# Selection columns moved into the unused columns of another constant tile, and every page of SBUF 32 bytes lower

## The chip, the cores and the metric

The kernel runs on one core of a Trainium2 chip. A core has a matrix engine (TensorE, PE in the profile), a vector engine (VectorE, DVE), a scalar engine (ScalarE, ACT), a general engine (GpSimd, POOL) and a queue engine (SyncE, SP), which run side by side and wait for one another by semaphores, and 16 DMA engines that move data between HBM and SBUF. SBUF is the working memory: 128 partitions, each a row of bytes; a tile takes the same byte addresses in all its partitions. The metric is the device time of one execution in microseconds (us), as the median of several; ns are nanoseconds. A clock of 1.00 in a row of the profile is the full clock of the matrix engine, 0.50 half of it.

## What is computed

Two layers over 1024 latent tokens of width 1024 and 256 context tokens, in float32. Layer 0 is windowed attention (16 query heads, 4 key/value heads of 128, a window of 128 tokens to each side, all context keys and one sink logit in the same softmax), layer 1 a convolution module (three projections, a gate, a depthwise convolution of 31 taps, a layer norm, a projection back). Each layer has a modulation that comes from small vectors `c` and `c_ctx` through `ada_w`.

```python
shift, scale, gate = split(silu_c @ ada_w[i] + ada_b[i], 3)
h_lat = rmsnorm(x, norm_g[i]) * (1 + scale) + shift
# layer 0
proj = h_lat @ w_in                 # q, k, v and a gate path z
p = softmax([sink, q @ kc, q @ k_window])
y = ((p_ctx @ vc + p_win @ v) * silu(z)) @ w_out
# layer 1
a, gl, z = split(h_lat @ w_in + b_in, 3)
u = depthwise_conv31(a * sigmoid(gl)) + dw_b
y = (silu(layernorm(u)) * silu(z)) @ w_out
x = x + gate * y                    # after each layer; at the end rmsnorm(x)
```

## The kernel before

The large products are made with float32r operands. Each factor is split into a high part (a copy in float32r, by ScalarE) and a low part (the rest, by VectorE or GpSimd), and `mm3` (L196) adds three matmuls: high by high, high by low, low by high. Nearly all of them have 128 x 128 weights and a moving operand of 512 columns. In the profile's names the moving operand stands first: `psg<-hh_page,whi_page` streams 512 columns of `hh_page` past the weights `whi_page` into the PSUM tile `psg`.

The stages, in order of time: up to about 41 us the modulation weights, tokens and first weights are loaded and the first vectors made (the matrix engine partly fills with matmuls of zeros, `spin`, L306); to 100 us the first projections; to 830 us attention head by head, with the projections of the next head filled in between; to 1010 us the projection back of layer 0; to 1500 us the convolution layer (VectorE and GpSimd do the taps, while the matrix engine does its projections); then the projection back and the output.

Memory. `cpool` holds constants and small tiles, `pgpool` the working pages: 45 pages of 1024 floats and 6 half pages of 528 floats (`Pages`, L54; L114 and L115), which are given out and taken back as the program goes on. In the built program tiles are laid one behind the other in the order of their first use, each rounded up to 32 bytes. The constants begin like this:

```python
    ident = ctile([P, P], F32, "ident")      # L161, 512 bytes in each partition, at 1152
    vt = ctile([P, P], F32, "vt")            # L162, 512 bytes, at 1664
    sel = ctile([P, 2], F32, "sel")          # L163, 8 bytes, takes 32, at 2176
    sink = ctile([P, NH], F32, "sink")       # L164, 64 bytes, at 2208
```

`ident` and `vt` lie at multiples of 64 bytes. `sel` takes 32 bytes, and the tiles behind it are odd multiples of 32: `ones` at 2336, `dww` at 2848, `pthi` and `ptlo` (the transposed probabilities, and later the buffers of the convolution) at 4832 and 16096, and all 45 pages and 6 half pages. A page is 4096 bytes and a half page 2112 bytes (33 x 64), so all of them lie 32 bytes past a multiple of 64. Of the pages 26 lie 32 bytes past a multiple of 256, 9 at 96, 6 at 160 and 4 at 224. Slices of them that the matrix engine reads begin at multiples of 512 bytes from a page's start.

`sel` holds two columns of ones and zeros. It is loaded once (L298) and read by the matrix engine as a moving operand of 5 rows and 2 columns, 32 times in all, when the modulation is turned into columns (`ada_cols`, L413). `vt` holds the columns of several vectors: columns 96 to 111 are written from the norm weights (L325), columns 0 to 95 later (`turn_vecs`); columns 112 to 127 are not used.

What sets the order: the instructions are written out in a fixed order, with a scheduler that orders some of the engines' work from an estimate of times; each engine then runs its list in order, and waits for semaphores.

Of the kernel before, what the change touches and what calls it, by code (L numbers as in the profile page):

```python
# [9 lines left out]
F32 = mybir.dt.float32  # L10
# [4 lines left out]
P = 128  # L15
# [79 lines left out]
def backbone_kernel(  # L95
# [47 lines left out]
    def ctile(shape, dt, name):  # L143
        return cpool.tile(shape, dt, tag=name, name=name, bufs=1)
# [15 lines left out]

    ident = ctile([P, P], F32, "ident")  # L161
    vt = ctile([P, P], F32, "vt")  # L162
    sel = ctile([P, 2], F32, "sel")  # L163
    sink = ctile([P, NH], F32, "sink")  # L164
    nsink = ctile([P, NH], F32, "nsink")
    ones = ctile([P, P], F32, "ones")
# [1560 lines left out]
```

## Time and profile before

| what | before |
|---|---|
| median of 3 runs | 1757.55 us (1756.67 to 1760.27) |
| span of the profiled execution | 1752.9 us |
| median less span | 4.6 us |
| TensorE busy | 1720.7 us, 98% of the span |
| VectorE, ScalarE, GpSimd busy | 66%, 51%, 51% |
| DMA | 242.45 MB, mean 138 GB/s |

The span runs from the first to the last instruction of the profiled execution; the device time of a run has a few microseconds around it. Busy time of the matrix engine is the time in which at least one matmul is under way. Matmuls overlap one another, so what one of them costs is the step from its start to the start of the next, not its own length: a chain row such as `5.54 PE psg L89 x24` says that 24 matmuls follow one another in 5.54 us. All instructions have the line of a helper (L89), so the groups are told apart by their tiles.

### The profile page before, as it was taken

How to read it: one execution, taken by the hardware profiler on the slowest of the kernel's cores; microseconds unless marked ns; L12 is line 12 of the kernel's file. 1: busy time of each engine (PE TensorE's matmuls, PEld its weight loads, DVE VectorE, ACT ScalarE, POOL GpSimd, SP SyncE). 2: the span in 40 equal slices, each digit the busy share in tenths (PEclk: the TensorE clock that was granted, in tenths of full speed). 3: DMA queues.
4: the chain of work that ended last, by engine and by line, in shares of the span. 5: the costliest groups of instructions: out<-in, count | busy, mean ns of one | idle time of the engine just before them, and what ended most of it. 6: DMA issues, size and time to landing. Idle time of an engine off the chain costs nothing.

```text
span 1752.9 us, 23877 instructions
## 1 busy us (share of the span) xinstructions
PE 1720.7 (98%) x8420; PEld 1424.8 (81%) x8420; DVE 1148.3 (66%) x2079; ACT 889.4 (51%) x1548; POOL 895.4 (51%) x705
## 2 busy tenths in 40 slices
PE   7999999999999999999999999999999999999997
PEld 4788888888888888888888888888888888788886
DVE  6755564556546563656315189999999999867823
ACT  7555553445345444545334355554665564466731
POOL 0245654566636565653101267998898888130300
PEclk9999999999999999999999999999999999999999
DMA  9334443444334542436777733011121202377971
GB/s 313 107 82 139 136 133 85 145 147 145 100 105 143 152 142 87 136 119 203 279 250 239 241 90 105 13 54 31 43 79 36 91 30 79 120 254 243 325 264 48
DMA packets 195324, 242.45 MB, mean 138 GB/s; under 512 B 11798, under 2 KB 126790, under 8 KB 195204
## 3 DMA queue, kind: packets, MB, share of 16 engines
q1 hardware_dynamic: 188516, 230.10, 40.3%
q10 hardware_dynamic: 6688, 10.83, 2.6%
q8 instruction: 66, 1.08, 0.3%
q14 instruction: 54, 0.44, 0.1%
HBM read 188.70 MB, written 41.69 MB: 131 GB/s over the span
## 4 chain that ended last, share of the span: by engine, by line
PE 86%; DMA 5%; DVE 3%; POOL 2%; ACT 2%; issue 2%; SPq 1%; ACTq 0%; POOLq 0%; DVEq 0%
PE psg L89 44%; PE pss L89 22%; PE pso L89 19%; DMA araw_page<-in_ada_w_dram 1%; POOL rope_half L89 1%; DMA low_page<-in_conv_w_out_dram 1%; DMA rope_half<-rope_half 1%; SPq L89 1%; DMA low_page<-in_attn_w_out_dram 1%; DMA wolC<-low_page 1%; DVE mask_page L89 1%; ACT p_page L89 0%; POOL wlo_page L89 0%; POOL low_page L89 0%; DMA wraw_page<-in_attn_w_in_dram 0%
## 5 line engine op out<-in xcount | busy, mean ns | idle before, releaser
L89 POOL TENSOR_TENSOR odd_half<-odd_half,prod_half 128x513 f32<-128x513 f32 (+2 forms) x252 | 312.8, 1250 | 24.2 <-ACT prod_half L89 11.0
L89 PE MATMUL psg<-hh_page,whi_page 128*128 128x512 f32 x600 | 237.6, 396 | 0.0
L89 PE MATMUL psg<-hh_page,wlo_page 128*128 128x512 f32 x600 | 236.9, 395 | 0.0
L89 PE MATMUL psg<-hl_page,whi_page 128*128 128x512 f32 x600 | 236.8, 395 | 0.0
L89 POOL TENSOR_TENSOR wlo_page<-wraw_page,whi_page 128x1024 fp32r<-128x1024 f32 x70 | 173.1, 2475 | 104.1 <-ACT whi_page L89 83.2
L89 ACT ACTIVATE prod_half<-ubuf,dww 128x513 f32<-128x513 f32 (+2 forms) x252 | 165.1, 674 | 107.3 <-POOL odd_half L89 105.1
L89 POOL TENSOR_SCALAR p_page<-p_page,sc 128x640 f32<-128x640 f32 (+1 forms) x128 | 100.8, 787 | 224.4 <-DVE sc L89 208.7
L89 PE MATMUL psg<-h2h_page,whi_page 128*128 128x512 f32 x464 | 183.9, 396 | 0.0
L89 PE MATMUL psg<-h2h_page,wlo_page 128*128 128x512 f32 x464 | 183.0, 394 | 0.0
L89 PE MATMUL psg<-h2l_page,whi_page 128*128 128x512 f32 x464 | 182.4, 393 | 0.0
L89 DVE SCALAR_TENSOR_TENSOR pss<-ubuf,dww,pss 128x512 f32<-128x512 f32 (+3 forms) x270 | 172.3, 670 | 0.1
L89 DVE SCALAR_TENSOR_TENSOR pss<-ubuf,wsum,pss 128x512 f32<-128x512 f32 (+3 forms) x270 | 171.7, 670 | 0.2
L89 DVE TENSOR_TENSOR ptlo<-pss,pthi 128x640 fp32r<-128x640 f32 (+1 forms) x144 | 103.3, 717 | 64.0 <-ACT pthi L89 62.8
L89 ACT ACTIVATE p_page<-p_page,sc 128x641 f32<-128x641 f32 (+1 forms) x128 | 102.7, 802 | 74.1 <-DVE sc L89 69.7
L89 ACT ACTIVATE pthi<-pss 128x640 fp32r<-128x640 f32 (+1 forms) x144 | 88.6, 615 | 91.7 <-PE pss L89 86.3
L89 PEld LDWEIGHTS psg<-hh_page,wlo_page 128*128 128x128 f32 x600 | 112.9, 188 | 26.3
L89 PEld LDWEIGHTS psg<-hh_page,whi_page 128*128 128x128 f32 x600 | 113.0, 188 | 20.8 <-DVE kvc_page L89 0.2
L89 PEld LDWEIGHTS psg<-hl_page,whi_page 128*128 128x128 f32 x600 | 112.9, 188 | 20.7
L89 ACT ACTIVATE whi_page<-wraw_page 128x1024 fp32r<-128x1024 f32 x88 | 92.6, 1053 | 69.0 <-PE psg L89 25.5
L89 PE MATMUL pso<-h2l_page,whi_page 128*128 128x512 f32 x304 | 119.9, 394 | 0.0
L89 PE MATMUL pso<-h2h_page,whi_page 128*128 128x512 f32 x304 | 119.8, 394 | 0.0
L89 PE MATMUL pso<-h2h_page,wlo_page 128*128 128x512 f32 x304 | 119.6, 394 | 0.0
(244 smaller groups left out, 4105.2 us busy)
## 6 DMA issues: line engine op xcount, KB each, us to landing
wraw_page<-in_conv_w_in_dram SPq DMA_DIRECT2D x48, 512.0 KB
wraw_page<-in_attn_w_in_dram SPq DMA_DIRECT2D x40, 512.0 KB
wol_page<-wolA SPq DMA_DIRECT2D x32, 512.0 KB
wo_page<-in_attn_w_out_dram SPq DMA_DIRECT2D x32, 512.0 KB
wo_page<-in_conv_w_out_dram SPq DMA_DIRECT2D x32, 512.0 KB
wol_page<-wolC SPq DMA_DIRECT2D x32, 512.0 KB
rope_half<-rope_half ACTq DMA_DIRECT2D x80, 128.0 KB
araw_page<-in_ada_w_dram SPq DMA_DIRECT2D x32, 256.0 KB
```

Of the source, the lines that this page charges most:

```text
L89: r = f(*a, **k)
```

## The change

The tile `sel` is no longer made; the name now stands for two of the unused columns of `vt`. The load at L298 and the reads in `ada_cols` are written as before.

```diff
     ident = ctile([P, P], F32, "ident")
     vt = ctile([P, P], F32, "vt")
-    sel = ctile([P, 2], F32, "sel")
+    sel = vt[:, 112:114]
     sink = ctile([P, NH], F32, "sink")
     nsink = ctile([P, NH], F32, "nsink")
     ones = ctile([P, P], F32, "ones")
```

In the built program the instructions of every engine and of both DMA queues stand in the same order as before, with the same operands and the same semaphores waited for, but that `sel` reads `vt`. What differs is the addresses. `sel` is at 2112 in place of 2176, both multiples of 64. All tiles behind it lie 32 bytes lower: `sink` at 2176, `ones` at 2304, `dww` at 2816, `pthi` and `ptlo` at 4800 and 16064, and all 45 pages and 6 half pages at multiples of 64 bytes. Of the pages 26 are now at multiples of 256, 9 at 64 past one, 6 at 128 and 4 at 192. The distances between any two tiles behind `sel` are as before. Of the small tiles that follow `ptlo`, those that were at multiples of 64 are now 32 past one.

## The prediction

> **What bounds the kernel now.** I read the head of the page first, then the busy time by stage, the waits of the matrix engine and the chain of work that ended last.
>
> ```profile
> span 1752.9 us, 23877 instructions
> PE 1720.7 (98%) x8420; PEld 1424.8 (81%) x8420; DVE 1148.3 (66%) x2079; ACT 889.4 (51%) x1548; POOL 895.4 (51%) x705
> ```
>
> The matrix engine works for 98% of the span. By stage, with the columns window, its length, busy time and instructions of PE, PEld, DVE, ACT, POOL, the granted clock, the DMA share and GB/s:
>
> ```profile
> 0.00:41.00 41.00, 32.73 (x129) 18.48 (x129) 24.54 (x43) 29.83 (x36) 0.92 (x7) 0.96 0.98 310
> 100.00:830.00 730.00, 723.28 (x3992) 623.83 (x3991) 410.77 (x811) 353.60 (x754) 405.40 (x333) 1.00 0.43 129
> 830.00:1010.00 180.00, 180.00 (x834) 147.83 (x833) 52.70 (x102) 65.70 (x93) 24.27 (x26) 1.00 0.75 255
> 1010.00:1500.00 490.00, 488.51 (x2127) 396.69 (x2126) 463.35 (x752) 278.62 (x403) 407.88 (x300) 1.00 0.19 58
> 1500.00:1739.46 239.46, 239.41 (x1050) 194.68 (x1049) 148.29 (x275) 125.63 (x197) 42.58 (x28) 1.00 0.64 220
> ```
>
> From 100 us on it leaves out 8.3 us in 1639. Only the first 41 us are set by DMA (share 0.98); there the matrix engine spins on zeros. Its longest waits, and the chain in the convolution stage (start, length, what):
>
> ```profile
> PE pso L89 <- DVE alo_page L89: 4.7, 5, 2.2
> PE pss L89 <- DVE ptlo L89: 3.6, 2, 3.2
> ```
>
> ```profile
> 1169.76 5.57 PE pso L89 x24
> 1175.32 5.57 PE psg L89 x24
> 1180.89 5.54 PE pso L89 x24
> 1186.43 5.54 PE psg L89 x24
> ```
>
> Nothing waits here but for the matmul before. So the time of this kernel is the step from one matmul to the next, some 231 to 232 ns for 512 columns, times their number; and a change of addresses counts if it changes that step, or the first 41 us.
>
> **The change part by part.** *The tile that goes.* The instructions, their order and their waits are the same on every engine, so no instruction and no wait is added or taken away. The load and the readers of the selection columns:
>
> ```profile
> L89 PE MATMUL pso<-sel,arow_half x32: 245/247/268, 16.4 to 59.6; 5*128 5x2 f32 x32
> L89 SPq DMA_DIRECT2D sel<-in_k_sel_dram x1: 417/417/417, 2.4 to 2.4; - x1
> ```
>
> The DMA writes the same 8 bytes per partition, into another tile; the 32 small matmuls read from a multiple of 64 bytes before and after. Other columns of `vt` are written by VectorE, but no wait was added for that. I take 0, and the whole DMA issue, 0.4 us, is the most that it could give or cost.
>
> *VectorE and ScalarE at other addresses.* The taps of the convolution read the same buffer at starting points that move on by 4 bytes from one instruction to the next, so they cover nearly all places within 64 bytes. Durations as least/median/most, from 1160 to 1480 us:
>
> ```profile
> L89 ACT ACTIVATE prod_half<-ubuf,dww x163: 707/727/732, 1159.5 to 1477.9; 128x513 f32<-128x513 f32 x163
> L89 DVE SCALAR_TENSOR_TENSOR pss<-ubuf,wsum,pss x174: 476/744/750, 1162.8 to 1479.8; 128x512 f32<-128x512 f32 x168, 128x256 f32<-128x256 f32 x6
> ```
>
> The 163 ScalarE instructions lie within 3.4%, and the median stands near the top (the 476 of VectorE are its 256 columns). An address that is not a multiple of 64 costs these engines nothing that can be seen, and the matrix engine covers them: 0. GpSimd's reads are nearly all at one alignment, so it is not shown there; a gain or a loss of a few per cent is covered as well (it is busy for 408 of 490 us in its fullest stage).
>
> *DMA.* Where DMA sets the end, the chain has these pieces:
>
> ```profile
> 6.40 5.91 DMA araw_page<-in_ada_w_dram
> 15.91 7.07 DMA araw_page<-in_ada_w_dram
> 27.19 6.19 DMA araw_page<-in_ada_w_dram
> 33.40 5.10 DMA araw_page<-in_ada_w_dram
> ```
>
> Together 24.27 us. All pages lie 32 past a multiple of 64, so no row shows a large aligned transfer. For a bound I take the rate at a full share: 310 / 0.98 = 316 GB/s in the first stage against 255 / 0.75 = 340 between 830 and 1010 us, where rows are longer. If alignment were worth that whole 7%, 1.7 us would go; if it costs as much, 1.7 us come. Between such ends I take 0, since no row ties the rate to an address.
>
> *The matrix engine's reads.* This is the term that matters, and no large matmul of this trace has its moving operand at a multiple of 64. What can be seen is that the full clock is not used to the full. Matmuls of 512 columns at half clock (start, length) and the windows of that time, of a run of zeros, of a second such run, and of the convolution:
>
> ```profile
> 28.60 0.63 PE L89 MATMUL pss<-hh_page,wlo_page 128*128 128x512 f32 x1
> 29.03 0.63 PE L89 MATMUL pso<-ahi_page,c 128*4 128x512 f32 x1
> 29.46 0.63 PE L89 MATMUL pso<-alo_page,c 128*4 128x512 f32 x1
> 29.88 0.55 PE L89 MATMUL pso<-ahi_page,c 128*4 128x512 f32 x1
> ```
>
> ```profile
> 28.60:29.88 1.28, 1.28 (x4) 0.33 (x3) 1.28 (x2) 0.99 (x1) 0.00 (x0) 0.50 1.10 348
> 17.72:21.35 3.63, 3.63 (x18) 3.00 (x16) 2.44 (x10) 3.22 (x6) 0.00 (x0) 1.00 1.11 343
> 23.27:23.97 0.70, 0.70 (x4) 0.56 (x3) 0.00 (x0) 0.70 (x2) 0.00 (x0) 1.00 1.11 334
> 1100.00:1480.00 380.00, 380.00 (x1644) 308.81 (x1643) 365.39 (x540) 224.71 (x304) 338.12 (x238) 1.00 0.16 50
> ```
>
> A window's count takes in neighbours that reach into it; the weight loads (PEld) count the steps: 3 in 1.28 us is 427 ns at clock 0.50. Twice the clock would give 213.3. The convolution has 380.00 / 1643 = 231.3 ns, that is 18.0 ns or 7.8% more; the zeros had 3.63 / 16 = 226.9 at one time and 0.70 / 3 = 233 at another. So at the full clock the stream is held up by something, and other engines' work does not seem to be it: the steps are as long in the convolution, with VectorE at 96%, as between 830 and 1010 us with VectorE at 29%. Whether it has to do with the 32 bytes, this trace bears on at one place. The transposed probabilities are streamed in pieces of 128 columns that lie apart, each of 512 bytes and each beginning and ending in the middle of 64 bytes, and the queries in one piece:
>
> ```profile
> L89 PE MATMUL pss<-kh_page,ql_page 128*128 128x384 f32 x96 | 32.5, 339 | 0.0
> L89 PE MATMUL pso<-ptlo,vh_page 128*128 128x384 f32 x64 | 21.4, 335 | 0.0
> ```
>
> Three pieces touch 27 stretches of 64 bytes, one piece of 384 columns 25, and the three pieces are not slower (335 against 339 ns, length of one). Torn ends thus cost nothing that can be seen. What stays possible is that each 64 bytes within the stream cost more for being read across a boundary; I take 0 for it, as the row nearest to the question speaks for 0, and keep both ends: 18.0 ns less for each 512 columns, and 2 ns more (231.3 to the 233 of the second run of zeros).
>
> [...]
>
> *The sum.* 1752.9 + 0 + 0 + 0 is the span; the median of the runs stands 4.6 us above it. Forecast: 1757.5 us, and within no change 1754 to 1761.
>
> **The rivals.** *First: the 32 bytes are what holds the stream up, and it goes wholly.* For: the excess is there at the full clock only, and every stream lies off a multiple of 64. Against: the pieces above. The price goes by stage. In the attention stage some of the time is transposes:
>
> ```profile
> L89 PE MATMUL pss<-ident,p_page 128*128 128x128 f32 x608 | 87.2, 273 | 0.5 <-POOL p_page L89 0.5
> 92.99 0.44 PE pso L89 x4
> ```
>
> These take 0.44 / 4 = 0.11 us a step, just over twice 213.3 / 4, so they hardly suffer; 608 of them are 67 us, and 656 remain. A step of a transpose is 3 ns over its 106.7, and I leave as much on each matmul: 15 of 231.3 ns, 6.5%, would go. That is 43 us in attention, 12 in 830 to 1010, and 16 behind 1500. In the convolution it would be 32, but VectorE is busy for 463 of 490 us and becomes the bound; I take 18. In all 89 us: 1668. Without the 3 ns it would be 7.8% and 27 us at most in the convolution: 51 + 14 + 19 + 27 = 111 us, 1646, the utmost.
>
> [...]
>
> *Second: part of it goes.* The run of zeros at 226.9 ns shows that the same addresses allow 1.9% less than 231.3. If every stream went that well, (656 + 180 + 489 + 239) x 1.9% = 30 us: 1728. For: it has been seen. Against: the second run of zeros, at the same addresses, had 233, so it is not the address alone.
>
> [...]
>
> **How the numbers follow.** No change has 0.38: nothing but addresses moves, and the two engines whose reads can be told apart by address show no regard for it. The first rival has 0.22 and the second 0.20, since the excess of 18 ns is real and has no cause in the trace. The third has 0.20, for the same reason. A measurement of this kernel can tell about 0.2% from no change. Faster is 0.42, same 0.38, slower 0.20. The range reaches from 1660, just below the first rival, to 1766; what lies out are the worse part of the third rival and the utmost of the first, 0.17 together.
>
> **What would show it.** Steps in the convolution (380.00 us in 1643 weight loads): 231.3 says no change, 227 the second rival, 216 the first, with VectorE near 100% and waits of the matrix engine on it; 233 the third. The four DMA pieces at 24.3 us within 1.7. ScalarE's 727 ns and VectorE's 744 stay. The forecast is wrong if the step moves by 0.5 ns or more, or if a wait of the matrix engine appears that is not in the list.

## The result and the profile after

| | before | after |
|---|---|---|
| median, 20 runs each | 1756.84 us (1753.52 to 1760.51) | 1754.92 us (1751.98 to 1757.54) |
| ratio | | 0.9992 (0.9985 to 0.9998) |
| span of the profiled execution | 1752.9 us | 1753.0 us |

The time is the same within the 0.2% that can be told from no change. Inside that bound there is a small gain of 1.9 us in the medians, whose interval ends just short of 1. A second comparison gave 0.9989 (0.998 to 0.9997).

The head of the page after, and its stages, with the columns as in the prediction (window, length, PE, PEld, DVE, ACT, POOL, clock, DMA share, GB/s):

```profile
span 1753.0 us, 23877 instructions
PE 1721.8 (98%) x8420; PEld 1423.6 (81%) x8420; DVE 1142.9 (65%) x2079; ACT 890.2 (51%) x1548; POOL 896.3 (51%) x705
```

```profile
0.00:41.00 41.00, 33.69 (x129) 18.74 (x129) 25.18 (x44) 29.61 (x36) 0.92 (x7) 0.92 0.97 313
830.00:1010.00 180.00, 180.00 (x834) 147.62 (x834) 52.89 (x103) 65.10 (x93) 24.25 (x26) 1.00 0.74 255
1010.00:1500.00 490.00, 488.51 (x2127) 396.11 (x2126) 463.13 (x752) 278.61 (x403) 408.41 (x300) 1.00 0.19 58
1100.00:1480.00 380.00, 380.00 (x1643) 308.35 (x1642) 365.27 (x539) 224.50 (x304) 338.04 (x238) 1.00 0.16 50
```

In these two stages as many matmuls go through as before: 834 of 834 in the projection back of layer 0, 2127 of 2127 in the convolution. (From 100 to 830 us there are 3985 against 3992; in other profiles of the two kernels that number goes from 3988 to 4003.) The step in the convolution is 380.00 / 1642 = 231.4 ns; it was 231.3. The chain in the convolution reads as it did:

```profile
1169.55 5.57 PE pso L89 x24
1175.12 5.57 PE psg L89 x24
1180.68 5.54 PE pso L89 x24
1186.22 5.54 PE psg L89 x24
```

The other engines' instructions there (least/median/most in ns), and the load and the readers of the selection columns:

```profile
L89 ACT ACTIVATE prod_half<-ubuf,dww x163: 707/726/734, 1159.3 to 1477.7; 128x513 f32<-128x513 f32 x163
L89 DVE SCALAR_TENSOR_TENSOR pss<-ubuf,wsum,pss x174: 471/745/755, 1162.6 to 1479.6; 128x512 f32<-128x512 f32 x168, 128x256 f32<-128x256 f32 x6
L89 PE MATMUL pso<-vt,arow_half x32: 246/246/267, 17.2 to 57.7; 5*128 5x2 f32 x32
L89 SPq DMA_DIRECT2D vt<-in_k_sel_dram x1: 417/417/417, 2.4 to 2.4; - x1
```

726 against 727 ns, 745 against 744, 246 against 247, 417 against 417. And the pieces of DMA in the chain of the first 41 us:

```profile
6.41 5.79 DMA araw_page<-in_ada_w_dram
15.46 6.84 DMA araw_page<-in_ada_w_dram
28.95 5.96 DMA araw_page<-in_ada_w_dram
35.84 5.29 DMA araw_page<-in_ada_w_dram
```

Together 23.88 us, 0.39 less than before.

### The profile page after: what moved, and what is told of

The parts are those of the page before. It is cut to its first block, busy times and chain, and to the rows that moved or that the text cites. A ratio compares the mean times of both kernels' runs of the same rounds, so it can differ in the third digit from the quotient of the medians.

```text
span 1753.0 us, 23877 instructions
## 1 busy us (share of the span) xinstructions
PE 1721.8 (98%) x8420; PEld 1423.6 (81%) x8420; DVE 1142.9 (65%) x2079; ACT 890.2 (51%) x1548; POOL 896.3 (51%) x705
## 4 chain that ended last, share of the span: by engine, by line
PE 84%; DMA 6%; DVE 3%; POOL 2%; issue 2%; ACT 2%; SPq 1%; ACTq 0%; POOLq 0%; DVEq 0%
PE psg L89 43%; PE pss L89 21%; PE pso L89 19%; DMA araw_page<-in_ada_w_dram 1%; DMA rope_half<-rope_half 1%; POOL rope_half L89 1%; DMA wraw_page<-in_attn_w_in_dram 1%; SPq L89 1%; DMA low_page<-in_conv_w_out_dram 1%; DMA low_page<-in_attn_w_out_dram 1%; POOL wlo_page L89 0%; DMA x_page<-in_x_dram 0%; DVE mask_page L89 0%; DMA wolC<-low_page 0%; DMA wo_page<-in_conv_w_out_dram 0%
```

## The experiments

Three questions were left. Is the matrix engine's step deaf to every address, or only to this shift? What does its excess over 213 ns (the 427 ns at clock 0.50, halved: an estimate) consist of? And where do the two microseconds come from?

**The changed kernel again, and the 32 bytes put back.** The first is the changed kernel, run again. The second adds an unused tile of 32 bytes, so that every page is where it was before, while the selection columns stay in `vt`.

> The changed kernel itself, beside the runs that follow. If the 0.08% between it and the kernel before is real: ratio 0.9985 to 0.9998 again. If it is the scatter of the runs: 1.000 within 0.0007. In both, the step of a 512-column matmul in the convolution stays at 231.3 ns (380 us in 1642 or 1643 weight loads between 1100 and 1480 us).

```diff
     sel = vt[:, 112:114]
+    pad = ctile([P, 8], F32, "pad")
```

> The selection columns stay in the other tile, and an unused tile of 32 bytes puts every later tile back to where it was (pages 32 bytes past a multiple of 64). If addresses give the small gain: ratio to the kernel before 1.000, and the DMA pieces of the first 41 us as before (24.3 us). If the merging of the tiles gives it: 0.999. If it was scatter: 1.000 here and in the changed kernel alike. Step 231.3 ns by every theory.

The changed kernel had 1754.17 us against 1755.98, ratio 0.9989 (0.998 to 0.9997); with the 32 bytes put back 1756.37, ratio 1.0 (0.9991 to 1.0009). The convolution with the bytes put back:

```profile
1100.00:1480.00 380.00, 380.00 (x1643) 308.86 (x1642) 365.22 (x541) 225.61 (x307) 337.93 (x239) 1.00 0.16 50
```

1642 loads, as with the changed kernel. So the two addresses give the same step, and moving `sel` by itself gives nothing within 0.09%. If the gain of 0.1% is real, it goes with the addresses, though not with the step.

**Half of the pages off, and all of them off by 4 bytes.** The pages are made 32 bytes longer and used from an offset on. With offset 0 they alternate between multiples of 64 (24 of 45) and 32 past one; with one float they lie 4 bytes past a multiple of 32.

```diff
-        t = self.pool.tile([P] + list(shape or [self.words]), dt, tag=f"{self.tag}{i}",
-                           name=f"{name}_{self.tag}_{self.count}", bufs=1)
+        t = self.pool.tile([P, self.words + SLACK], dt, tag=f"{self.tag}{i}",
+                           name=f"{name}_{self.tag}_{self.count}", bufs=1)[:, OFF:OFF + self.words]
+        if shape and len(shape) > 1:
+            names = "abc"[:len(shape)]
+            t = t.rearrange(f"p ({' '.join(names)}) -> p {' '.join(names)}", **dict(zip(names[1:], shape[1:])))
```

`SLACK` is 8; `OFF` is 0 in the first kernel and 1 in the second. The first is thus the control of the second: the pages lie as far apart, and only the 4 bytes differ.

> Pages of 4128 bytes in place of 4096 (the last 32 not used), so that 24 of 45 lie at a multiple of 64 and 21 at 32 past one: the control of the next run, and a mixture of both alignments in one trace. If addresses do not matter to the matrix engine: steps of 231 to 232 ns whether the stream is from one sort of page or the other, ratio 0.999 to 1.001. If 32 bytes mattered to it in any way: two groups of steps more than 1 ns apart.

> The same pages, used from their fifth byte on, so that every page lies 4 bytes past a multiple of 32 and no stream, load or packet begins at a multiple of 16. My theory (the matrix engine does not care where a stream begins): step 231.3 ns within 0.5, ratio to the kernel before 0.999 to 1.002. Rival (lines of 16 bytes, which 32 and 64 do not test): each stream crosses one line more in every 16 bytes or at its ends, step 232 to 240 ns, ratio 1.003 to 1.04. For DMA: if packets care for alignment, the first 41 us grow by 1 us or more and the packets' share of the first stage rises; if not, they stay.

The first had 1758.73 us, ratio 1.0009 (0.9998 to 1.002). The second had 1784.62, ratio 1.0155 (1.014 to 1.0171): 27 us slower by the ratio, 25.9 by the medians of the two. The convolution of the first, and then of the second:

```profile
1100.00:1480.00 380.00, 380.00 (x1640) 307.55 (x1639) 365.50 (x540) 224.86 (x305) 337.20 (x239) 1.00 0.16 49
```

```profile
1100.00:1480.00 380.00, 380.00 (x1609) 303.85 (x1608) 360.10 (x536) 219.12 (x301) 332.39 (x241) 1.00 0.16 47
```

With 4 bytes the step is 380.00 / 1608 = 236.3 ns, 4.9 longer than in the changed kernel and 4.5 longer than in the control (380.00 / 1639 = 231.9). The profile has 5993 matmuls of 512 columns with 128 x 128 weights; 5993 x 4.5 ns = 27 us, which is the loss. The control itself has 1639 loads, where all ten profiles with the pages of the kernel before or of the changed kernel have 1642 or 1643: with other distances between the pages the step is some 0.4 ns longer, and no run shows why. So the matrix engine does heed the address of its operands, only not in steps of 32 bytes.

**The stream by itself.** Groups of 24 equal matmuls behind the changed kernel's own work, in one execution of each kernel; nothing reads their results. Each operand has a page of its own, at a multiple of 64. The first kernel varies the kind of stream:

```diff
+        def group(mov, wt, rows=P):
+            for _ in range(24):
+                PE.matmul(o[0:rows], wt, mov, start=True, stop=True)
+        group(m["warm"][:, 0:512], w[:, 0:P])
+        group(m["base"][:, 0:512], w[:, 0:P])
+        group(m["four"][:, 1:513], w[:, 0:P])          # 4 bytes on
+        group(m["late"][:, 8:520], w[:, 0:P])          # 32 bytes on
+        group(m["narrow"][:, 0:512], w[:, 0:4], 4)     # 4 columns of weights
+        group(m["strided"][:, 0:1024:2], w[:, 0:P])    # every second float
+        group(m["same"][:, 0:1].to_broadcast([P, 512]), w[:, 0:P])
+        group(b[:, 0:512], wb[:, 0:P])                 # bfloat16
```

> The changed kernel with 192 matmuls more at its end, whose results are not used: eight groups of 24, each streaming 512 columns of a tile of its own past weights of 128 columns. After a group that warms up the clock: from a multiple of 64; 4 bytes past it; 32 bytes past it; past weights of 4 columns only; every second float; the same float 512 times; and in bfloat16. My theory (the stream at full clock is held up by how fast float32r operands can be read, whatever the address): 231 ns within 3 in the first three, 231 with narrow weights, 460 or so with every second float if lines are what is read, under 220 with the same float 512 times, 216 in bfloat16. Rival (weights loaded in between hold it up): 231 in the first three, 214 to 220 with narrow weights. Rival (alignment holds it up): 214 to 220 from a multiple of 64, 231 or more in the other two. Rival (something behind the array, the writing of 4-byte results): 231 in all but bfloat16, and there too.

The matrix engine's timeline there (start, length of the whole group; each name ends in the operand's):

```profile
1745.60 5.76 PE L90 MATMUL pss<-benwarm_page,benw_page 128*128 128x512 f32 x24
1751.20 5.76 PE L90 MATMUL pss<-benbase_page,benw_page 128*128 128x512 f32 x24
1756.80 5.92 PE L90 MATMUL pss<-benfour_page,benw_page 128*128 128x512 f32 x24
1762.56 5.76 PE L90 MATMUL pss<-benlate_page,benw_page 128*128 128x512 f32 x24
1768.15 5.72 PE L90 MATMUL pss<-bennarrow_page,benw_page 128*4 128x512 f32 x24
1773.70 11.04 PE L90 MATMUL pss<-benstrided_page,benw_page 128*128 128x512 f32 x24
1784.55 5.44 PE L90 MATMUL pss<-bensame_page,benw_page 128*128 128x512 f32 x24
1789.83 5.35 PE L90 MATMUL pss<-benhalf_page,benv_page 128*128 128x512 bf16 x24
```

From start to start, divided by 24: 233 ns in the first group as in the second, so no warming of the clock shows; 233 at a multiple of 64 and 233 at 32 bytes past it, 240 at 4 bytes; 231 with 4 columns of weights; 452 where every second float is read; 220 where one float is read over and over. For bfloat16 the next start is missing; if its last matmul reaches as far beyond the next start as in the first two groups (5.76 - 5.60 = 0.16 us), it has 5.19 / 24 = 216 ns, an estimate. So most of the excess over 213 goes with reading different floats: 13 of some 20 ns go when the address stands still (220 for 233), and all but about 3 with operands of half the size (216, the estimate). It is not the writing, since the groups at 220 and at 216 write the same tile of 4-byte results as those at 233. Loading fewer weight columns gives 2 ns at most (231 for 233).

The next two kernels vary the place. One has 8, 12 and 16 bytes, weights moved by 4 bytes, and 256 columns side by side and 16 bytes apart:

> Eight groups of 24 matmuls stand behind the changed kernel's own work; nothing reads their results, and the time of the whole is longer by them. From the start of one group to the start of the next, divided by 24: streams of 512 columns at 0, 8, 12 and 16 bytes past the start of a page, then the first of these again with its weights 4 bytes past the start of a page, then 256 columns one after the other, and 256 columns of which each lies 16 bytes behind the last. Theory (the stream is read in stretches of 16 bytes): 233 ns at 0 and at 16 bytes, 240 at 8 and 12; weights at 4 bytes leave 233; 256 columns take 117, and with 16 bytes between them four times as many stretches are read, 4 x 117 = 468 at the utmost. Rival (stretches of 32 bytes): 240 at 16 bytes as well, and the last group no more than twice the group before it. Rival (the weights carry the loss at 4 bytes): 240 in the group with the moved weights.

```profile
1747.78 5.76 PE L90 MATMUL pss<-benbase_page,benw_page 128*128 128x512 f32 x24
1753.38 5.76 PE L90 MATMUL pss<-beneight_page,benw_page 128*128 128x512 f32 x24
1758.98 5.71 PE L90 MATMUL pss<-bentwelve_page,benw_page 128*128 128x512 f32 x24
1764.53 5.78 PE L90 MATMUL pss<-bensixteen_page,benw_page 128*128 128x512 f32 x24
1770.15 5.74 PE L90 MATMUL pss<-benbase_page,benv_page 128*128 128x512 f32 x24
1775.72 2.99 PE L90 MATMUL pss<-benfour_page,benw_page 128*128 128x256 f32 x24
1778.55 5.75 PE L90 MATMUL pss<-benstrided_page,benw_page 128*128 128x256 f32 x24
```

In this order: 233, 233, 231, 234, 232 with moved weights, 118 for 256 columns, and about 233 for 256 columns that lie 16 bytes apart (again with 0.16 us taken off). Weights moved by 4 bytes cost nothing (232 for 233). My theory that the engine fetches stretches of 16 bytes and pays for each of them fails at two places: 8 and 12 bytes lose nothing, and columns 16 bytes apart cost 0.91 ns each, hardly more than the 0.88 of columns 8 bytes apart. The other kernel asks for the period:

> Eight groups of 24 matmuls behind the changed kernel's own work, their results read by nothing: streams of 512 columns that start 0, 4, 12, 20, 28 and 36 bytes past the start of a page (a multiple of 64), 4 bytes again in another page, and 128 columns that lie 32 bytes apart. Start to start, divided by 24. Theory (4 bytes past a multiple of 32 is the place that costs): 240 ns at 4, 36 and again at 4, and 231 to 234 at 0, 12, 20, 28. Rival (4 past a multiple of 16): 240 at 20 too. Second rival (an odd multiple of 4 past 8): 240 at 12, 20 and 28 too, so that the 231 seen at 12 was an accident. Third rival (the 240 belonged to one page, whatever the offset): 232 at the second group with 4. The last group, by columns that stand apart at 0.89 to 0.91 ns each: 116 ns; by stretches of 16 or 32 bytes that are longer to reach: more.

```profile
1742.47 5.76 PE L90 MATMUL pss<-benwarm_page,benw_page 128*128 128x512 f32 x24
1748.06 5.92 PE L90 MATMUL pss<-benfour_page,benw_page 128*128 128x512 f32 x24
1753.82 5.72 PE L90 MATMUL pss<-bentwelve_page,benw_page 128*128 128x512 f32 x24
1759.38 5.88 PE L90 MATMUL pss<-bentwenty_page,benw_page 128*128 128x512 f32 x24
1765.10 5.70 PE L90 MATMUL pss<-entwentyeight_page,benw_page 128*128 128x512 f32 x24
1770.64 5.84 PE L90 MATMUL pss<-benthirtysix_page,benw_page 128*128 128x512 f32 x24
1776.32 5.83 PE L90 MATMUL pss<-benagain_page,benw_page 128*128 128x512 f32 x24
1781.99 2.82 PE L90 MATMUL pss<-benstrided_page,benw_page 128*128 128x128 f32 x24
```

At 0: 233 ns; at 4, 20, 36 and again 4: 240, 238, 237 and 236; at 12 and 28: 232 and 231. The first rival holds: what counts is the place within 16 bytes. Four past a multiple of 16 costs 3 to 7 ns, twelve past it saves 1 to 2. The two groups at 4 bytes differ by 4 ns between themselves, so one or two ns in a single group prove little; what 12 bytes are worth is for the whole kernel to show. The last group, 128 columns that lie 32 bytes apart, has about 112 ns (0.12 us taken off), 0.88 ns a column: a wider distance is not dearer. The expectation for it was 116.

**The best place, in the kernel.** The same edit with `OFF` 3 and with `OFF` 7, so that all pages lie 12 and 28 bytes past a multiple of 32. The control is again the kernel with `OFF` 0.

> As the kernel with pages 4 bytes past a multiple of 32, but 12 bytes past it. Theory (only 4 bytes past costs): steps of 512 columns of 231.7 ns and the time of the kernel before, ratio 0.999 to 1.001. Rival (any start that is no multiple of 16 costs): steps of 236 and ratio 1.015 as at 4 bytes.

> As the kernel with pages 12 bytes past a multiple of 32, but 28 bytes past it, which is 12 past a multiple of 16 too. Theory (the matrix engine's streams repeat every 16 bytes, and 12 past a multiple of 16 is their best start): steps of 512 columns of 230.0 ns on the mean, 1654 weight loads in the 380 us of the convolution, ratio 0.994 as at 12 bytes. Rival (12 bytes past a multiple of 32 is a place of its own): 231.7 ns, 1643, ratio 1.000. Second rival (the gain at 12 bytes had another cause than the streams, such as the start-up or the transfers): ratio below 0.997 with steps of 231.7 ns, or 1.000 with steps of 230.0.

At 12 bytes 1746.7 us, ratio 0.9943 (0.993 to 0.9957); at 28 bytes 1748.17, ratio 0.9951 (0.994 to 0.9963). The first, which was expected to change nothing, and then the second:

```profile
PE 1712.4 (98%) x8420; PEld 1426.3 (82%) x8420; DVE 1142.9 (65%) x2079; ACT 888.3 (51%) x1548; POOL 895.4 (51%) x705
1100.00:1480.00 380.00, 380.00 (x1655) 311.34 (x1654) 366.65 (x544) 224.22 (x304) 341.07 (x239) 1.00 0.17 50
```

```profile
PE 1709.6 (98%) x8420; PEld 1422.7 (81%) x8420; DVE 1149.8 (66%) x2079; ACT 888.9 (51%) x1548; POOL 897.4 (51%) x705
1100.00:1480.00 380.00, 380.00 (x1657) 310.98 (x1656) 367.99 (x543) 223.61 (x303) 340.90 (x239) 1.00 0.17 52
```

Steps of 380.00 / 1654 = 229.7 and 380.00 / 1656 = 229.5 ns, 1.7 and 1.9 below 231.4. With 5993 of them that is 10 and 11 us. Against the control the steps are 2.1 and 2.3 ns shorter and the medians 12.0 and 10.6 us. The busy time of the matrix engine fell by 9.4 and 12.2 us against the changed kernel, and the medians by 9.3 and 8.7 against the kernel before. Some of it is given back: span less busy time is 1747.9 - 1712.4 = 35.5 and 1746.6 - 1709.6 = 37.0 us, against 31.2 in the changed kernel. These are the fastest kernels of this study.

**Where the two microseconds come from.** The first profiles of both addresses parted at one place. In the start-up the matrix engine waits for the low part of a modulation page (a matmul of the third set, `pso<-alo_page,c`). Before, this wait was 2.21 us and ended at 43.09; the clock then fell to 0.50 for 3 us. In the two first profiles of the changed kernel it was 1.4 to 1.5 us, ended at 42.4, and the clock stayed at 1.00. That is some 2 us by 50 us, the size of the gain. Two tests: eight further matmuls in the kernel before, meant for this gap, so that the engine isn't idle there (their result is read by nothing), and one more profile of each kernel.

```diff
                 for n, (c, r) in enumerate(parts):
+                    if (pr, i, k, n) == (1, 2, 0, 1):
+                        fill = ps_o(1)
+                        for _ in range(8):
+                            PE.matmul(fill[0:4], c[:, 2 * i + k, :], parts[0][1][:, k], start=True, stop=True)
```

> The kernel before, with eight further matmuls of the second set of modulation rows in the gap of 2.21 us that the matrix engine has at 40.9 to 43.1 us; their result is read by nothing, and every other instruction is as before. Theory (the gap brings the clock down): the clock stays at 1.00 between 41 and 52 us, no step of 427 ns is left between 43 and 48 us, the wait ends at 43.1 as before, and what follows is 1.3 us earlier: the median is 1.3 us below the kernel before if the lead is kept to the end (ratio 0.9993), and equal if waits further on take it. Rival (the clock falls for another reason, at its own time): 0.5 between 44 and 47 us as before, ratio 1.000. Second rival (the changed addresses alone make the lead): the clock stays up, but the time is not below that of before.

> The kernel before, a second time, to see whether its start-up is the same in another execution. Theory (pages at 32 past a multiple of 64 bring the third set of transfers in later): the wait of the matrix engine for the low part of the third page ends at 43.1 to 43.3 us, as in both kernels with such pages so far, and the clock falls to 0.5 behind it. Rival (chance, from one execution to the next): it ends anywhere from 42.0 to 43.3, and the clock falls only where it ends late.

> The changed kernel, a third time, as a partner of the kernel before in the same hour. Theory (addresses): the same wait ends at 42.4 us, as in its two profiles so far, and the clock stays at 1.00. Rival (chance): anywhere from 42.0 to 43.3.

The eight matmuls did not come into the gap. The condition names the second set, and the gap stands in the third. In the matrix engine's timeline of that kernel, the matmuls added to the second set, and the end of the wait:

```profile
32.66 2.24 PE L89 MATMUL pso<-ahi_page,c 128*4 128x512 f32 x9
44.51 0.39 PE L89 MATMUL pso<-alo_page,c 128*4 128x512 f32 x1 [1.05 <-DVE alo_page L89]
```

So this run is no test of a filled gap. The time was 1758.14 us, ratio 1.0013 (1.0002 to 1.0024): 2.1 us more, about what eight steps of 0.23 us come to. The clock stayed at 1.00 behind the wait, which was 1.05 us here, and yet no time was won.

The kernel before, in its second profile: the end of that wait in the matrix engine's timeline, and the window behind it.

```profile
42.36 0.39 PE L89 MATMUL pso<-alo_page,c 128*4 128x512 f32 x1 [1.60 <-DVE alo_page L89]
44.00:47.00 3.00, 3.00 (x17) 2.33 (x15) 2.76 (x4) 3.00 (x6) 1.30 (x1) 1.00 1.01 397
```

The changed kernel, in its third:

```profile
43.19 0.40 PE L89 MATMUL pso<-alo_page,c 128*4 128x512 f32 x1 [2.49 <-DVE alo_page L89]
44.00:47.00 3.00, 3.00 (x8) 1.65 (x7) 1.95 (x4) 2.38 (x4) 1.29 (x1) 0.50 1.02 403
```

The roles are exchanged: this time the kernel before was early and kept its clock, and the changed kernel was late and lost it. The theory falls; this wait differs from one execution to the next. It doesn't set the end either: the changed kernel's third profile, with the late start, has the shortest span of the three, 1750.9 us. And a start-up at the full clock is not yet a run at the full clock. In the first profile of the changed kernel, which kept it there, the clock fell for 3.4 us later on; the same window in the first profile of the kernel before stands below it:

```profile
590.00:593.40 3.40, 3.40 (x10) 2.73 (x10) 2.23 (x4) 2.60 (x6) 3.40 (x3) 0.50 0.27 77
590.00:593.40 3.40, 2.11 (x11) 1.93 (x12) 2.67 (x7) 3.30 (x7) 1.60 (x2) 1.00 0.16 45
```

The kernel before had the same fall in its second profile; the mean granted clock is 0.995 in both profiles. Over all runs the mean granted clock is alike: 0.9962 in 29 runs of the kernel before, 0.9964 and 0.9963 in 20 and 11 of the changed kernel.

So the cause of the 0.1% stays open. It isn't the step of the matrix engine, it isn't the start-up wait, and it is hardly the clock (0.0002 of 1753 us is 0.4 us). One thing does go with the addresses: the transfers from SBUF to SBUF (queue q10) took 2.6 to 2.7% of the span in four profiles with pages at 32 past a multiple of 64, and 2.5% in the three of the changed kernel; the mean time of their 5120 packets of 2048 bytes was 137 to 141 ns and 131 to 133 ns. Those for `rope_half` have some 1% of the chain that ended last, 18 us; 4% of that is under 1 us, an estimate, so they could give a part of it. Whether the matrix engine's waits in the attention stage follow from that, single profiles can't tell, since their spans scatter by 3 us (1750.9 to 1753.9 for the changed kernel).

## Why the prediction was right, and where its reasons were not

*The forecast.* 1757.5 us with no change; 1754.92 came, inside 1754 to 1761 and with a ratio within 0.2% of 1. No change was the forecast but had a chance of only 0.38, against 0.42 for faster. The 4.6 us added to the span were too many: in every run on record the time is 1.7 to 1.9 us above the span of the same execution. The rest came of setting the profiled execution, a fast one, against the median of others.

*The tile that goes: 0.* The load stayed at 417 ns and the readers at 246; with the 32 bytes put back the ratio was 1.0. Right.

*VectorE and ScalarE: 0.* 745 against 744 ns and 726 against 727. Right. Even pages 4 bytes off a multiple of 32 left VectorE's busy time in its scatter (1147.0 us against 1142.9 to 1149.8 elsewhere), as far as such a sum can say.

*DMA: 0, within 1.7 us.* The four pieces took 23.88 us for 24.27. Right in size for the loads, and with pages 4 bytes past a multiple of 32 the first 41 us still moved 308 GB/s, against 310 before and 313 after. That no row ties a transfer to an address was true of the one trace; the packets from SBUF to SBUF, which the sum left out, became some 4% shorter (137 to 141 ns before, 131 to 133 after).

*The matrix engine's reads: 0.* 231.4 against 231.3 ns. Right, and for the reason given from the torn pieces: beginning and ending inside 64 bytes cost nothing there (335 against 339 ns). The reason given with the chances was too wide: that VectorE and ScalarE "show no regard" for an address was taken to speak for the matrix engine, which does show regard, with 4.9 ns lost at 4 bytes past a multiple of 16 and 1.7 to 1.9 gained at 12. The change was neutral as both 0 and 32 are multiples of 16: the streams at 0, 16 and 32 bytes took 233, 234 and 233 ns.

*First and second rival (1668, 1728).* The first gave the whole excess of 18 ns to the 32 bytes, the second a part of it. The step moved by 0.1 ns. In the groups the excess goes with reading different floats, at every address: 220 ns with one float and about 216 with bfloat16. Together they had 0.42, more than the forecast itself; that was the misjudged part of the prediction. The best address found takes off less than 2 of the 18 ns.

*Third rival (1769).* Each step was to go from 231.3 to the 233 ns of the second run of zeros, 11 us in all, since the reads of a stream and of the next weights would meet more often. That was the author's supposition, which had 0.20 and bears on the upper end of the range, 1766; no run shows such meetings. The step stayed at 231.4 ns, and weights moved by 4 bytes left 232 ns. The distances between pages do not change here; in the kernel where they do (`OFF` 0) the step is 231.9 ns, though whether weights and stream meet there is not shown.

*What would show it.* The list of signs named steps of 231.3, the DMA pieces and the two durations; all stood as listed for no change. A step of 229.5, which two of these kernels have, lay between the signs for no change and for the second rival, and the prediction had no case for it.

## What to carry to other kernels

Where the chain is one matmul behind the other, price a change of addresses by the step, counted as weight loads in a fixed window; 24 equal matmuls behind the kernel's own work show a difference of several ns in one profile (240 against 233 here), before anything is moved. In this kernel the start of the float32r streams within 16 bytes was what counted (steps of 231.4 ns at 0, 236.3 at 4, 229.7 at 12), and a shift by 32 bytes gave 0.1 ns; try 12. And before a difference between two profiles is made a cause, take each kernel's profile again: here a wait that explained the gain to the microsecond had changed sides. And look in the trace where an added instruction ran, before its result is read: here eight of them stood in another gap than the one they were meant for.

## What the runs showed of the hardware

- At the full clock, a float32r stream of 512 columns took 231 to 234 ns at 0, 8, 12, 16 and 32 bytes past a multiple of 64, 236 to 240 ns at 4 past a multiple of 16, and 220 ns with one float repeated. In the whole kernel, pages at 12 past a multiple of 16 gave 229.5 to 229.7 ns. Why 12 is best, no run shows.
- Columns 8, 16 and 32 bytes apart took 0.88, 0.91 and 0.88 ns each (452 ns for 512, 233 for 256, 112 for 128), against 0.45 for neighbours (233 for 512).
- In the start-up the matrix engine's clock was 0.50, 0.61 and 0.50 on the mean from 44 to 47 us, behind idle gaps of 2.21, 2.36 and 2.49 us, and 1.00 there behind gaps of 1.05 to 1.62 us, at the same place in the program. Some of the latter runs have a fall later: 0.50 from 590.0 to 593.4 us in the first profile of the changed kernel, 0.91 on the mean from 60 to 80 us with pages at 28 bytes.
- SBUF-to-SBUF packets of 2048 bytes took 137 to 141 ns on the mean with pages at 32 past a multiple of 64, and 131 to 133 ns with pages at multiples of 64; what makes them longer, no run shows.
